# Three small edits late in a hybrid attention, gated-linear-attention and convolution layer: which engine makes the low parts of the last four output weights, what four weight scalings are queued behind, and which engine does one scaling of the end

## The chip, the cores and the metric

One Trainium2 chip; the kernel runs on one of its cores. The time is the device time of one execution in microseconds. The executions shown of the kernel before took 885.99, 885.36 and 882.93 us, median 885.36. A further execution was recorded by the hardware profiler; rows and times inside the kernel are from that one, and are microseconds from the start of its span.

## The reference, cut to what matters

One layer over 512 latent tokens (width 1024) with 256 context tokens. The edits touch the output projection `w_out`, the weights of `w_down`, and the final RMSNorm.

```python
h = modulate(rms_norm(x_lat, norm1_g), sh1, sc1)
mix = token_mixer(h, hc, ...)            # ends in (g_mla*br_mla + g_gla*br_gla) @ w_out
x_lat = x_lat + gt1 * mix
h = modulate(rms_norm(x_lat, norm2_g), sh2, sc2)
val, gate = split(h @ w_up)              # 2 x 2816 columns
gate = depthwise_conv_3x3(gate) + conv_b
x_lat = x_lat + gt2 * ((gelu(gate) * val) @ w_down)
return rms_norm(x_lat, final_g)
```

## The kernel before

**Matrix products in three parts.** Every float32 operand is split into a high part, rounded to the narrower `F32R`, and a low part, the rest. `split` (line 141) does it with a cast on ScalarE and a subtraction on GpSimd or VectorE; `mm3` (146) multiplies high by high, high by low and low by high, so each product is three matmuls on TensorE.

**Who sets the order.** The code is written in the order of the mathematics. A scheduler then puts each engine's instructions into one fixed sequence, from its own estimate of when each becomes ready; on the chip an engine works through its sequence and waits at an instruction whose inputs are not there. `tc.issue_after(x)` tells the scheduler to put what is traced in its block behind `x` on the engine of `x`; instructions of the block on other engines get no such rule. Loads are issued by SyncE's queue (SP), in order as well. A load waits there until the last reader of the buffer that it overwrites is done: three buffers `raw`, two `rawd`, and four pairs `whi`/`wlo` of split weights, which TensorE frees by finishing with them.

**The output projection** (lines 1359 to 1450). `load_wo` loads eight blocks of 128 rows of `w_out` (k = 0 to 7) and splits each into its own pair of tiles `s`. Blocks 4 to 7 are the last; their low parts are made by GpSimd for 4 and 6, by VectorE for 5 and 7. `w_out_norm(t)` then multiplies them with the 128 tokens of tile t, adds the result to the residual (`x`), normalizes it into `xn`, and `transposed(t, xn)` turns `xn` on TensorE and makes `h` for the MLP.

**The down projection** (lines 1570 to 1680). Eighteen of the 22 blocks of `w_down` go through a Strassen-like scheme in nine pairs (n = 0 to 8). For each n, the loop at 1619 loads and splits two weight tiles, `wa` and `wb`, and does 24 matmuls (`product`, 1581). The other four blocks (`last`) are multiplied plainly at the end; before that each is scaled by `gt2` and split. These four scalings stand in the loop's passes n = 1, 2, 4 and 5 in an `issue_after` block behind `done[0]`, a matmul, while the block holds work for VectorE and ScalarE alone. After the loop come the sums `u1`, `u2`, `u7`, `c22` and nine passes of `back`, whose first weights (`back_weights(0)`) are traced at n = 6.

**The end** (lines 1710 to 1762). For each tile t of 128 tokens: twelve matmuls per half with the four `last` blocks, the residual added from PSUM on VectorE, squares on ScalarE with their sum, the product with the gain `fg` on GpSimd, a reciprocal root `r2`, and a scaling of each half of 512 columns by `r2`. Tile 3 is cut into 512, 256 and 256 columns, the last quarter in a bank of its own.

Of the kernel before, what the change touches and what calls it, by code (L numbers as in the profile page):

```python
# [13 lines left out]
ALU = mybir.AluOpType  # L14
# [58 lines left out]
def block_kernel(ctx: ExitStack, tc: tile.TileContext, p, out):  # L73
# [3 lines left out]
    class Engine:  # L77
# [5 lines left out]
        def __getattr__(self, op):  # L83
            fn = getattr(self.eng, op)

            def call(*args, **kw):
                if self.name in behind:
                    with tc.issue_after(behind[self.name].ins):
# [6 lines left out]
    V, A, G, PE, SY = (Engine("V", nc.vector), Engine("A", nc.scalar), Engine("G", nc.gpsimd),  # L95
                       Engine("PE", nc.tensor), Engine("SY", nc.sync))
    cnt = [0]

    def tl(pool, shape, dt, tag, bufs=None):
        cnt[0] += 1  # L100
        kw = {} if bufs is None else {"bufs": bufs}
        return pool.tile(shape, dt, name=f"{tag}_{cnt[0]}", tag=tag, **kw)
# [8 lines left out]
    def pb():  # L111
        return tl(psp, [128, 512], F32, "pb", 4)
# [4 lines left out]
    def S4(shape, dt=F32R):  # L117
        return tl(s4, shape, dt, "s4")

    def S4f():  # L120
        return S4([128, 1024], F32)

    def sm(n, tag, bufs=2):
        return tl(small, [128, n], F32, tag, bufs)
# [4 lines left out]
    def whl():  # L129
        return tl(st, [128, 1024], F32R, "whi", 4), tl(st, [128, 1024], F32R, "wlo", 4)  # L130

    def f(ap):
        return ap.bitcast(F32)

    def tt(eng, out_, a, b, op):
        return eng.tensor_tensor(out=out_, in0=a, in1=b, op=op)

    def sub(eng, out_, a, b):
        eng.tensor_tensor(out=out_, in0=a, in1=b, op=ALU.subtract)

    def split(hi, lo, src, eng=None):

        A.copy(hi, src)
        sub(eng or G, lo, src, f(hi))

    def mm3(o, sh, sl, mh, ml, first, last):
        PE.matmul(o, lhsT=sh, rhs=mh, start=first, stop=False)
        PE.matmul(o, lhsT=sh, rhs=ml, start=False, stop=False)
        return PE.matmul(o, lhsT=sl, rhs=mh, start=False, stop=last)
# [67 lines left out]
    def split_w(r, n=1024, eng=None):  # L217
        h, l = whl()
        split(h[:, 0:n], l[:, 0:n], r[:, 0:n], eng)
        return h, l  # L220
# [125 lines left out]
    with tc.tile_pool(name="e1", bufs=1) as e1:  # L346
# [324 lines left out]
        for j in range(1, 8):  # L671
            n = j + 1
# [351 lines left out]
        for k in range(2):  # L1024
            V.scalar_tensor_tensor(out=kc[:, 256 * k:256 * k + 256], in0=cb_[k], scalar=col("kv_norm_g", k),
                                   in1=rb[:, 0:256], op0=ALU.mult, op1=ALU.mult)
# [332 lines left out]
    def load_wo(k, tile_=raw_tile):  # L1359
        r = tile_()  # L1360
        load[0] = SY.dma_start(out=r, in_=w_out[:, k, :])
        h_, l_ = S4([128, 1024]), S4([128, 1024])
        split(h_, l_, r, V if k in (5, 7) else G)
        wo.append((h_, l_))

    def up_weights(i):
        return split_w(load_cols(w_up, FF + i * 128)), split_w(load_cols(w_up, i * 128))
# [8 lines left out]
    with tc.tile_pool(name="emg", bufs=1) as em_:  # L1376
# [9 lines left out]
        for j in range(8):  # L1386
# [16 lines left out]
            if j in (1, 2, 3, 5):  # L1403
                load_wo(len(wo), mraw)
# [76 lines left out]
        for c0 in (FF + 256, 256):  # L1481
            h_, l_ = S4([128, 1024]), S4([128, 1024])
# [13 lines left out]
    with tc.tile_pool(name="eff", bufs=1) as ef:  # L1496
# [55 lines left out]
        for i in range(3, NF):  # L1552
            w = up_weights(i)
            ps = (pb(), pb())
# [9 lines left out]
            n = (i - 4) // 2  # L1564
# [10 lines left out]
        def raw_():  # L1575
            raws[0] += 1
            return raw_tile() if raws[0] % 5 in (1, 2, 3) else tl(ef, [128, 1024], F32, "rawd", 2)

        done = [None]

        def product(ps, hl, c, w, b, start, stop):
            for t in range(2):
                cs, bs = slice(c + t * 128, c + t * 128 + 128), slice(b, b + 512)
                done[0] = mm3(ps[t], hl[0][:, cs], hl[1][:, cs], w[0][:, bs], w[1][:, bs], start, stop)

        def halves(z):
            return [z[:, 0:512], z[:, 512:1024]]
# [31 lines left out]
        for n in range(NP):  # L1619
            r = raw_()  # L1620
            SY.dma_start(out=r[:, 0:512], in_=w_down[:, 2 * n, 0:512])
            SY.dma_start(out=r[:, 512:1024], in_=sums_[n][:, 1536:2048])
            wa = split_w(r, eng=G if n < 2 else V)
            r = raw_()
            SY.dma_start(out=r, in_=sums_[n][:, 0:1024])
            wb = split_w(r, eng=G if n < 2 else V)
            a, z = n == 0, n == NP - 1
            product(p1, first[n], 0, wa, 0, a, z)
            product(p6, first[n], 768, wa, 512, a, z)
            product(p7, first[n], 512, wb, 512, a, z)  # L1630
            product(p5, first[n], 256, wb, 0, a, z)
            if n == 0:
                for k in range(NF - NL, NF):
                    last.append(S4f())
                    load[0] = SY.dma_start(out=last[-1], in_=w_down[:, k, :])
            elif n in (1, 2, 4, 5):
                r = last[len(wl_)]
                with tc.issue_after(done[0].ins):
                    tt(V, r, r, gt2, ALU.mult)
                    wl_.append((S4([128, 1024]), S4([128, 1024])))  # L1640
                    split(*wl_[-1], r, V)
            if n == NP - 3:
                bw.append(back_weights(0))
# [58 lines left out]
        def down(k, t, half, w, a=0, n=512):  # L1702
            cs, hs = slice(t * 128, (t + 1) * 128), slice(half * 512 + a, half * 512 + a + n)
            mm3(acc[t][half][:, a:a + n], hid[k][:, 0, cs], hid[k][:, 1, cs], w[0][:, hs], w[1][:, hs], k == NF - NL,
                k == NF - 1)

        def residual(t, a, b, ps):
            tt(V, x2[t][:, a:b], x2[t][:, a:b], ps, ALU.add)

        for t in range(4):  # L1710
            last = t == 3
            o_t = S4f()
            parts = [(0, 512), (512, 768), (768, 1024)] if last else [(0, 512), (512, 1024)]
            ss = sm(len(parts), f"ssf{len(parts)}")
            if not last:
                for half in range(2):
                    for n in range(NL):
                        down(NF - NL + n, t, half, wl_[n])
            for i, (a, b) in enumerate(parts):
                if not last:  # L1720
                    residual(t, a, b, acc[t][i])
                elif i == 0:
                    for n in range(NL):
                        down(NF - NL + n, t, 0, wl_[n])
                    residual(t, a, b, acc[t][0])
                elif i == 1:
                    for n in range(NL):
                        down(NF - NL + n, t, 1, wl_[n], 0, 256)
                    residual(t, a, b, acc[t][1][:, 0:256])
                else:  # L1730

                    cs = slice(t * 128, (t + 1) * 128)
                    rest = pb()[:, 0:256]
                    for n in range(NL):
                        hd, w = hid[NF - NL + n], wl_[n]
                        mm3(rest, hd[:, 0, cs], hd[:, 1, cs], w[0][:, a:b], w[1][:, a:b], n == 0, n == NL - 1)
                    residual(t, a, b, rest)
                if last and i == 2:
                    V.scalar_tensor_tensor(out=o_t[:, a:b], in0=x2[t][:, a:b], scalar=1.0, in1=x2[t][:, a:b], op0=ALU.mult,
                                           op1=ALU.mult, accum_out=ss[:, i:i + 1])  # L1740
                else:
                    A.activation(o_t[:, a:b], x2[t][:, a:b], AF.Square, accum_out=ss[:, i:i + 1])
                if not last or i == 0:
                    tt(G, x2[t][:, a:b], x2[t][:, a:b], fg[:, a:b], ALU.mult)
            s1 = sm(1, "ssg")
            tt(V, s1, ss[:, 0:1], ss[:, 1:2], ALU.add)
            if last:
                V.tensor_scalar(out=s1, in0=s1, scalar1=-0.5 / D, scalar2=-0.5 * EPS, op0=ALU.mult, op1=ALU.add)
                v = sm(1, "rv1")
                V.scalar_tensor_tensor(out=v, in0=ss[:, 2:3], scalar=-0.5 / D, in1=s1, op0=ALU.mult, op1=ALU.add)  # L1750
                r2 = rstd_exp(None, 1, None, v)
            else:
                r2 = rstd_exp(s1, 1, 1.0 / D)
            for i in range(2):
                hs = slice(512 * i, 512 * i + 512)
                if last and i == 1:
                    V.scalar_tensor_tensor(out=x2[t][:, hs], in0=x2[t][:, hs], scalar=r2, in1=fg[:, hs], op0=ALU.mult,
                                           op1=ALU.mult)
                elif t == 2:
                    V.tensor_scalar(out=x2[t][:, hs], in0=x2[t][:, hs], scalar1=r2, scalar2=None, op0=ALU.mult)  # L1760
                else:
                    A.activation(x2[t][:, hs], x2[t][:, hs], AF.Copy, scale=r2)
                (A if last and i == 0 else SY).dma_start(out=out[0, t * 128:(t + 1) * 128, hs], in_=x2[t][:, hs])
# [24 lines left out]
```

## Time and profile before

| what | before |
|---|---|
| time of the executions shown | 885.99, 885.36, 882.93 us (median 885.36) |
| time of the profiled execution | 884.84 us |
| its span | 882.9 us |
| mean granted TensorE clock | 0.997 |
| ScalarE (ACT), GpSimd (POOL) busy | 47%, 44% of the span |
| VectorE (DVE) busy | 73% of the span |

The profiled execution's time is 1.9 us more than its span, which runs from the first to the last instruction. In a row of the timeline stand the start, the duration, the engine, line and operation, the tile written and those read, a count of merged instructions, and in square brackets how long the engine stood idle before it and what it waited for. PE is TensorE, SPq the queue that issues loads. Nearly all rows carry line 90, the helper that records every instruction, so tiles tell the instructions apart: `s` is a tile of the large pool, `p` and `pb` are PSUM tiles.

### The profile page before, as it was taken

The numbers are of one execution on the slowest core, as the hardware profiler recorded it, in microseconds if no ns is written. First come the engines' busy times: TensorE is split into PE (matmuls) and PEld (weight loads), VectorE is DVE, ScalarE is ACT, GpSimd is POOL, SyncE is SP. The second block draws the span as 40 slices with busy tenths as digits, with TensorE's granted clock in tenths as the row PEclk, the third lists the DMA queues.
The fourth block names the chain that finished last, engine by engine and source line by source line (L and its number), as shares of the span: only waits on it lengthen the run. The fifth ranks groups of instructions, "written<-read, shape, count | busy, mean of one in ns | idle before, by whom it ended". The sixth has DMA issues, their size and how long they took to land.

```text
span 882.9 us, 12813 instructions
## 1 busy us (share of the span) xinstructions
PE 866.2 (98%) x4794; PEld 737.3 (83%) x4794; DVE 645.3 (73%) x1049; ACT 413.5 (47%) x666; POOL 385.3 (44%) x258
## 2 busy tenths in 40 slices
PE   7999999999999999999999999999999999999996
PEld 6788899888888888888887889888888888878885
DVE  4477788885978787985676684976677665787856
ACT  4455766773354545444544433333334333365414
POOL 2512355460524252434563422777767776400004
PEclk9999999999999999999999999999999999999998
DMA  9970001207414333536981721656546755588502
GB/s 294 320 183 1 1 4 33 73 27 213 107 37 131 109 108 84 168 107 217 288 275 56 225 96 37 227 180 193 188 142 194 225 181 158 163 278 271 212 12 95
DMA packets 141648, 130.53 MB, mean 148 GB/s; under 512 B 7947, under 2 KB 122995, under 8 KB 141586
## 3 DMA queue, kind: packets, MB, share of 16 engines
q1 hardware_dynamic: 140354, 126.67, 47.0%
q10 hardware_dynamic: 832, 2.40, 0.7%
q8 instruction: 37, 0.61, 0.3%
q0 software_dynamic: 400, 0.65, 0.3%
q14 instruction: 25, 0.20, 0.1%
HBM read 115.87 MB, written 13.63 MB: 147 GB/s over the span
## 4 chain that ended last, share of the span: by engine, by line
PE 86%; DVE 3%; DMA 3%; issue 3%; POOL 2%; ACT 2%; SPq 0%; POOLq 0%; DVEq 0%; ACTq 0%
PE pb L90 46%; PE p L90 20%; PE pb L89 14%; PE p L89 6%; DMA raw<-in_w_ada_dram 2%; POOL wlo L90 1%; DVE s L90 1%; POOL s L90 1%; DMA s<-in_w_down_dram 1%; ACT P L90 1%; DVE mx L90 1%; DVE kT L90 0%; ACT ph L90 0%; ACT s L90 0%; DVE P L90 0%
## 5 line engine op out<-in xcount | busy, mean ns | idle before, releaser
L90 POOL TENSOR_TENSOR wlo<-raw,whi 128x1024 fp32r<-128x1024 f32 (+1 forms) x91 | 210.9, 2325 | 217.8 <-ACT whi L90 187.3
L90 PE MATMUL pb<-s,whi 128*128 128x512 f32 (+1 forms) x906 | 271.6, 382 | 0.0
L90 PEld LDWEIGHTS pb<-s,whi 128*128 128x128 f32 x906 | 167.4, 188 | 32.0
L90 PE MATMUL pb<-s,wlo 128*128 128x512 f32 (+1 forms) x453 | 172.9, 382 | 0.0
L90 ACT CAST whi<-raw 128x1024 fp32r<-128x1024 f32 (+1 forms) x106 | 102.9, 975 | 123.6 <-PE pb L90 56.2
L90 DVE SCALAR_TENSOR_TENSOR ac<-pb,cwT,ac 128x441 f32<-128x441 f32 (+2 forms) x160 | 110.9, 694 | 13.6 <-ACT ac L90 9.3
L89 PE MATMUL pb<-s,whi 128*128 128x512 f32 x320 | 101.3, 394 | 0.0
L90 PEld LDWEIGHTS pb<-s,wlo 128*128 128x128 f32 x453 | 85.2, 188 | 16.4
L90 PE MATMUL p<-s,s 128*128 128x512 f32 (+1 forms) x398 | 84.2, 365 | 1.2 <-POOL s L90 0.6
L90 PEld LDWEIGHTS p<-s,s 128*128 128x128 f32 x398 | 67.0, 189 | 13.8 <-DVE s L90 1.3
L89 PEld LDWEIGHTS pb<-s,whi 128*128 128x128 f32 x320 | 59.3, 188 | 11.5
L89 PE MATMUL pb<-s,wlo 128*128 128x512 f32 x160 | 62.9, 393 | 0.0
L90 PE MATMUL p<-whi,s 128*128 128x512 f32 x168 | 55.9, 394 | 0.0
L90 PE MATMUL pb<-whi,s 128*128 128x512 f32 x164 | 53.5, 391 | 0.0
L90 POOL TENSOR_TENSOR s<-s,edge 128x512 f32<-128x512 f32 x7 | 10.5, 1504 | 93.8 <-ACT s L90 93.8
L90 PE MATMUL pb<-s,s 128*32 128x128 f32 (+2 forms) x340 | 46.1, 319 | 0.7 <-DMA s<-in_w_ada_dram 0.7
L90 ACT ACTIVATE ac<-ac 128x512 f32<-128x512 f32 x22 | 13.9, 632 | 70.3 <-DVE ac L90 70.1
L90 DVE TENSOR_TENSOR pl<-pb,ph 128x512 fp32r<-128x512 f32 x48 | 33.0, 687 | 13.0 <-ACT ph L90 12.5
L90 PE MATMUL p<-kT,s 128*128 128x512 f32 (+1 forms) x192 | 41.2, 351 | 0.9 <-ACT P L90 0.9
L90 PEld LDWEIGHTS pb<-s,s 128*128 128x128 f32 (+1 forms) x340 | 36.1, 159 | 6.6 <-DVE rv L90 1.1
L90 PE MATMUL p<-s,whi 128*128 128x256 f32 (+1 forms) x156 | 38.6, 339 | 0.0
L90 ACT CAST ph<-pb 128x512 fp32r<-128x512 f32 x48 | 28.2, 587 | 20.7 <-PE pb L90 20.6
(274 smaller groups left out, 1670.8 us busy)
## 6 DMA issues: line engine op xcount, KB each, us to landing
raw<-in_w_up_dram SPq DMA_DIRECT2D x44, 512.0 KB, 4.8
raw<-in_w_in_dram SPq DMA_DIRECT2D x28, 512.0 KB, 4.1
rawd<-in_w_down_dram SPq DMA_DIRECT2D x22, 512.0 KB, 5.2
s<-in_w_ada_dram SPq DMA_DIRECT2D x20, 512.0 KB, 6.4
ws<-rawd SPq DMA_DIRECT2D x18, 512.0 KB, 5.7
raw<-in_w_ada_dram SPq DMA_DIRECT2D x10, 512.0 KB, 7.7
xn<-in_w_ada_dram SPq DMA_DIRECT2D x10, 512.0 KB, 5.3
wa<-in_w_ada_dram SPq DMA_DIRECT2D x8, 512.0 KB, 5.3
```

Of the source, the lines that this page charges most:

```text
L89: return fn(*args, **kw)
L90: ins = fn(*args, **kw)
```

## The change

Three edits, and what follows from them in the order.

```diff
     def sub(eng, out_, a, b):
-        eng.tensor_tensor(out=out_, in0=a, in1=b, op=ALU.subtract)
+        return eng.tensor_tensor(out=out_, in0=a, in1=b, op=ALU.subtract)
 
     def split(hi, lo, src, eng=None):
         A.copy(hi, src)
-        sub(eng or G, lo, src, f(hi))
+        return sub(eng or G, lo, src, f(hi))
...
         h_, l_ = S4([128, 1024]), S4([128, 1024])
-        split(h_, l_, r, V if k in (5, 7) else G)
+        split(h_, l_, r, V if k > 3 else G)
         wo.append((h_, l_))
...
             r = raw_()
             SY.dma_start(out=r, in_=sums_[n][:, 0:1024])
-            wb = split_w(r, eng=G if n < 2 else V)
+            wb = whl()
+            low = split(*wb, r, G if n < 2 else V)
...
-            elif n in (1, 2, 4, 5):
+            elif n in (3, 4, 6, 7):
                 r = last[len(wl_)]
-                with tc.issue_after(done[0].ins):
+                with tc.issue_after(low.ins):
                     tt(V, r, r, gt2, ALU.mult)
                     wl_.append((S4([128, 1024]), S4([128, 1024])))
                     split(*wl_[-1], r, V)
...
-                elif t == 2:
+                elif t == 2 and i == 0:
                     V.tensor_scalar(out=x2[t][:, hs], in0=x2[t][:, hs], scalar1=r2, scalar2=None, op0=ALU.mult)
                 else:
                     A.activation(x2[t][:, hs], x2[t][:, hs], AF.Copy, scale=r2)
```

**First place: the output projection.** On VectorE, `s_801`, `s_804`, `s_807` and `s_810` are the low parts of blocks 4, 5, 6 and 7:

```order
 L90 TENSOR_TENSOR s_403_2384<-s_403_2384,p_798_4747 128x512
 L90 TENSOR_TENSOR s_796_4739<-sg_4733,s_796_4739 128x512
+L90 TENSOR_TENSOR s_801_4757<-raw_4754,s_800_4756 128x1024
 L90 TENSOR_TENSOR s_804_4763<-raw_4760,s_803_4762 128x1024
+L90 TENSOR_TENSOR s_807_4769<-raw_4766,s_806_4768 128x1024
 L90 TENSOR_TENSOR s_403_2384<-s_403_2384,p_798_4747 128x512
 L90 TENSOR_TENSOR s_810_4775<-raw_4772,s_809_4774 128x1024
```

Two subtractions of 128x1024 have come to VectorE, ahead of and behind the one that was there; GpSimd has lost the same two. On TensorE, at the same place (`p_819` is token tile 0, `p_825` tile 1, `s_806` and `s_807` the high and low part of block 6):

```order
 L90 MATMUL p_819_4786<-s_806_4768,s_787_4674 128x512
+L90 MATMUL p_819_4786<-s_807_4769,s_787_4674 128x512
+L90 MATMUL p_819_4786<-s_806_4768,s_787_4674 128x512 x2
+L90 MATMUL p_819_4786<-s_807_4769,s_787_4674 128x512
+L90 MATMUL p_819_4786<-s_806_4768,s_787_4674 128x512
 L90 MATMUL p_825_4852<-s_718_4311,s_703_4230 128x512
 L90 MATMUL p_825_4852<-s_719_4312,s_703_4230 128x512
```

The rest of block 6 for tile 0 is now done at once, where thirteen matmuls of tile 1 stood ahead of it. Behind this, block 7 of tile 0 is finished five matmuls sooner, and the transposes of tile 0 stand five matmuls sooner.

**Second place: VectorE in the loop over n.** Before, from the low part of n = 2's `wa` (`wlo_7241`) on; `gt_404` marks the four scalings, `wlo_7247` is n = 2's `wb`, `wlo_7283` and `wlo_7289` are n = 3's two:

```order
L90 TENSOR_TENSOR wlo_7241<-rawd_7237,whi_7240 128x1024
L90 TENSOR_TENSOR s_1115_7137<-ac_7125,s_1115_7137 128x512
L90 TENSOR_TENSOR s_1129_7187<-s_1129_7187,gt_404_2389 128x1024
L90 TENSOR_TENSOR wlo_7247<-raw_7244,whi_7246 128x1024
L90 TENSOR_TENSOR s_1130_7189<-s_1130_7189,gt_404_2389 128x1024
L90 TENSOR_TENSOR s_1140_7234<-s_1129_7187,s_1139_7233 128x1024
L90 TENSOR_TENSOR s_1131_7191<-s_1131_7191,gt_404_2389 128x1024
L90 TENSOR_TENSOR wlo_7283<-raw_7279,whi_7282 128x1024
L90 TENSOR_TENSOR wlo_7289<-raw_7286,whi_7288 128x1024
L90 TENSOR_TENSOR s_1132_7193<-s_1132_7193,gt_404_2389 128x1024
```

After, from the same place; `wlo_7236` and `wlo_7242` are n = 2, `wlo_7273` and `wlo_7279` n = 3, `wlo_7315` and `wlo_7321` n = 4, `wlo_7357` n = 5:

```order
L90 TENSOR_TENSOR wlo_7236<-rawd_7232,whi_7235 128x1024
L90 TENSOR_TENSOR s_1115_7137<-ac_7125,s_1115_7137 128x512
L90 TENSOR_TENSOR wlo_7242<-raw_7239,whi_7241 128x1024
L90 TENSOR_TENSOR wlo_7273<-raw_7269,whi_7272 128x1024
L90 TENSOR_TENSOR wlo_7279<-raw_7276,whi_7278 128x1024
L90 TENSOR_TENSOR s_1129_7187<-s_1129_7187,gt_404_2389 128x1024
L90 TENSOR_TENSOR wlo_7315<-rawd_7311,whi_7314 128x1024
L90 TENSOR_TENSOR s_1152_7308<-s_1129_7187,s_1151_7307 128x1024
L90 TENSOR_TENSOR wlo_7321<-rawd_7318,whi_7320 128x1024
L90 TENSOR_TENSOR s_1130_7189<-s_1130_7189,gt_404_2389 128x1024
L90 TENSOR_TENSOR wlo_7357<-raw_7353,whi_7356 128x1024
```

No scaling stands ahead of n = 3's low parts any more; the four are spread behind the second low part of n = 3, 4, 6 and 7. On SP's queue the two loads of `back_weights(0)` have moved back as well: its block of `w_down` behind the load for `back_weights(1)`, and its stored sums behind the first sums of `back_weights(2)`.

**Third place: VectorE at the end.** `s_1208` is tile 2, `s_1209` tile 3, `ssg` and `ssf` its sums of squares:

```order
-L90 TENSOR_SCALAR s_1208_7549<-s_1208_7549,rr_1283_7979 128x512 x2
+L90 TENSOR_SCALAR s_1208_7549<-s_1208_7549,rr_1283_7979 128x512
 L90 TENSOR_TENSOR s_1209_7550<-s_1209_7550,pb_7852 128x256
+L90 TENSOR_TENSOR ssg_8037<-ssf_1287_7992 128x1
 L90 TENSOR_TENSOR s_1209_7550<-s_1209_7550,pb_8022 128x256
-L90 TENSOR_TENSOR ssg_8037<-ssf_1287_7992 128x1
+L90 TENSOR_SCALAR ssg_8037<-ssg_8037 128x1
 L90 SCALAR_TENSOR_TENSOR s_1286_7991,ssf_1287_7992<-s_1209_7550 128x256
-L90 TENSOR_SCALAR ssg_8037<-ssg_8037 128x1
```

One of two scalings of tile 2 is gone from VectorE, and stands on ScalarE between tile 3's first square and its second. The sum of the first two squares now stands ahead of the last addition from PSUM.

More of the change, by code (lines that the diff above doesn't have):

```diff
@@ L1577, in raw_ @@
             return raw_tile() if raws[0] % 5 in (1, 2, 3) else tl(ef, [128, 1024], F32, "rawd", 2)
-        done = [None]
         def product(ps, hl, c, w, b, start, stop):
@@ L1583, in product @@
                 cs, bs = slice(c + t * 128, c + t * 128 + 128), slice(b, b + 512)
-                done[0] = mm3(ps[t], hl[0][:, cs], hl[1][:, cs], w[0][:, bs], w[1][:, bs], start, stop)
+                mm3(ps[t], hl[0][:, cs], hl[1][:, cs], w[0][:, bs], w[1][:, bs], start, stop)
         def halves(z):
```

## The prediction

> **What bounds the kernel now.** I read the busy shares first, then TensorE's waits by releaser, then its timeline around each.
>
> ```profile
> span 882.9 us, 12813 instructions
> PE 866.2 (98%) x4794; PEld 737.3 (83%) x4794; DVE 645.3 (73%) x1049; ACT 413.5 (47%) x666; POOL 385.3 (44%) x258
> PE p L90 <- DVE s L90: 2.5, 2, 2.1
> PE p L90 <- DVE wlo L90: 0.9, 1, 0.9
> PE p L90 <- POOL s L90: 0.6, 1, 0.6
> 668.40 97.95 PE pb L90 x432
> ```
>
> TensorE is busy 98% of the span, so only its idle time and what stands behind its last matmul can go. Of the three waits only the last two (total, times, longest) lie where the change reaches. The last row, from the chain of waits, gives the undisturbed pace: 97.95 / 432 = 0.227 us from one matmul's start to the next. A row of n matmuls without a break thus takes (n - 1) x 0.227 plus the last one's own 0.39 us.
>
> **First part: the low parts of blocks 4 and 6.**
>
> ```profile
> 478.81 2.94 ACT L90 CAST s<-raw 128x1024 fp32r<-128x1024 f32 x3
> 479.93 2.39 POOL L90 TENSOR_TENSOR s<-raw,s 128x1024 fp32r<-128x1024 f32 x1 [8.03 <-ACT s L90]
> 480.83 2.57 DVE L90 TENSOR_TENSOR s<-raw,s 128x1024 fp32r<-128x1024 f32 x1 [1.21 <-ACT s L90]
> 481.37 0.39 PE L90 MATMUL p<-s,s 128*128 128x512 f32 x1
> 482.37 20.26 PE L90 MATMUL p<-s,s 128*128 128x512 f32 x88 [0.61 <-POOL s L90]
> 775.87 1.23 DVE L90 TENSOR_TENSOR wlo<-rawd,whi 128x1024 fp32r<-128x1024 f32 x1 [1.67 <-ACT whi L90]
> ```
>
> The three casts of blocks 4 to 6 start at 478.81 and end about 0.95 apart, the first at 479.9. GpSimd makes block 4's low part until 482.32, and TensorE, due at 481.37 + 0.23 = 481.60, starts at 482.37: 0.77 late. The idle figure in brackets is smaller, because a matmul counts as busy for 0.39 and the next starts after 0.23. The 88 matmuls take 20.26 where 87 x 0.227 + 0.39 = 20.14 were due, so restarting costs another 0.1. Loss: 0.9.
>
> VectorE stands idle from 479.6 to 480.83 (the 1.21 in its row) and needs 1.23 for such a subtraction, as the sixth row shows. With the change it does block 4 from 479.9 to 481.1, block 5 to 482.3, block 6 to 483.4. TensorE needs them at 481.6, 483.0 and 484.3 (6 and 12 matmuls after the first): slacks of 0.5, 0.7 and 0.9. **The 0.9 goes.** GpSimd's two subtractions of 2.39 leave a queue that nothing else waits in here.
>
> [...]
>
> What is late next? Block 7's cast, and the transposes of tile 0, five matmuls sooner now.
>
> ```profile
> 483.43 0.33 SPq L90 DMA_DIRECT2D raw<-in_w_out_dram  x1
> 487.04 1.05 ACT L90 CAST s<-raw 128x1024 fp32r<-128x1024 f32 x1 [5.29 <-DMA raw<-in_w_out_dram]
> 490.04 10.38 POOL L90 TENSOR_TENSOR wlo<-raw,whi 128x1024 fp32r<-128x1024 f32 x4 [4.38 <-ACT whi L90]
> 493.50 4.66 DVE L90 TENSOR_TENSOR x<-x,xn 128x512 f32<-128x512 f32 x2
> 500.66 0.75 DVE L90 TENSOR_SCALAR xn<-x,rr 128x1024 f32<-128x1024 f32 x1
> ```
>
> Block 7's load left at 483.43, when VectorE released block 5's buffer, and was cast 3.6 later. Now it takes block 4's buffer at 481.1, so its cast ends near 485.8; TensorE reaches it 26 matmuls after 481.60, at 487.5. Its low part is ready near 487.1 against 488.9. The transposes come 83 matmuls after 481.60, at 500.4. `xn` was ready at 501.41; the two additions ahead of it took 4.66 because GpSimd's four subtractions ran beside them. These now start some 1.6 sooner, since their loads wait for buffers that come free 1.6 to 2.3 sooner; so `xn` moves to about 499.8. The slack of 0.6 is the smallest that this edit leaves, and I take no loss; the worst is one more GpSimd operation in the way, 2.4.
>
> **Second part: the four scalings.**
>
> ```profile
> 777.92 1.23 DVE L90 TENSOR_TENSOR s<-s,gt 128x1024 f32<-128x1024 f32 x1 [0.22 <-DMA s<-in_w_down_dram]
> 779.06 1.22 DVE L90 TENSOR_TENSOR wlo<-raw,whi 128x1024 fp32r<-128x1024 f32 x1
> ...
> 782.47 1.22 DVE L90 TENSOR_TENSOR s<-s,gt 128x1024 f32<-128x1024 f32 x1
> 783.60 1.22 DVE L90 TENSOR_TENSOR wlo<-raw,whi 128x1024 fp32r<-128x1024 f32 x1
> 780.14 1.99 ACT L90 CAST whi<-raw 128x1024 fp32r<-128x1024 f32 x2
> 782.94 1.07 PE L90 MATMUL pb<-whi,s 128*128 128x512 f32 x4
> 784.88 0.50 PE L90 MATMUL p<-wlo,s 128*128 128x512 f32 x1 [0.87 <-DVE wlo L90]
> ```
>
> From 777.92 VectorE works without a gap, 1.14 from start to start, and reaches n = 3's first low part at 783.60, though its cast ended at 781.2. Ahead of it stand three scalings and one low part of theirs. TensorE was due at 782.94 + 4 x 0.227 = 783.85 and starts at 784.88: 1.03 late, and this first matmul takes 0.50 instead of 0.39. Loss: 1.1.
>
> With the new order VectorE goes on from n = 2's second low part to n = 3's. VectorE was done with the instruction before at 777.92 - 0.22 = 777.7; less the 0.9 of the first part, it starts at 776.8, and n = 3's two end at 779.2 and 780.3. TensorE needs them as the 74th and 86th matmul of the loop, where 783.85 was the 79th: at 783.85 - 5 x 0.227 - 0.9 = 781.8 and at 784.5. Their casts, no longer behind the cast of a scaled weight, wait only for buffers that n = 1 has left. Slack: over 2.
>
> ```profile
> 794.00 1.99 ACT L90 CAST whi<-raw 128x1024 fp32r<-128x1024 f32 x2
> 794.75 1.54 PE L90 MATMUL pb<-whi,s 128*128 128x512 f32 x5
> ```
>
> A second, hidden loss: these five matmuls take 1.54 where 4 x 0.227 + 0.39 = 1.30 were due, while the cast that they need ends at 795.0: 0.2. That cast (n = 5's `wb`) stood behind casts of scaled weights and moves up too. From n = 4 on, each new pair is limited by its buffers, which TensorE frees 36 matmuls (8.2) ahead of their next use; a cast and a low part need 1.0 + 1.2, and a scaling and a low part of a scaled weight between add 2.4. So **1.3 goes** in this part.
>
> **Third part: the end.**
>
> ```profile
> 864.14 11.19 PE L90 MATMUL pb<-s,s 128*128 128x512 f32 x60
> 873.73 0.49 DVE L90 TENSOR_SCALAR s<-s,rr 128x512 f32<-128x512 f32 x1
> 874.13 1.52 DVE L90 TENSOR_SCALAR s<-s,rr 128x512 f32<-128x512 f32 x1
> 875.57 0.74 DVE L90 TENSOR_TENSOR s<-s,pb 128x256 f32<-128x256 f32 x2
> 876.63 0.42 DVE L90 SCALAR_TENSOR_TENSOR s<-s 128x256 f32<-128x256 f32 x1
> 877.15 0.16 DVE L90 SCALAR_TENSOR_TENSOR rv<-ssf,ssg 128x1 f32<-128x1 f32 x1
> 874.02 1.34 POOL L90 TENSOR_TENSOR s<-s,edge 128x512 f32<-128x512 f32 x1 [1.43 <-ACT s L90]
> 871.13 1.32 ACT L90 ACTIVATE s<-s,rr 128x512 f32<-128x512 f32 x2
> 873.22 0.63 ACT L90 ACTIVATE s<-s 128x512 f32<-128x512 f32 x1 [0.44 <-DVE s L90]
> 876.01 0.42 ACT L90 ACTIVATE s<-s 128x256 f32<-128x256 f32 x1 [2.06 <-DVE s L90]
> ```
>
> TensorE ends at 875.33; the rest is one chain. VectorE's second scaling takes 1.52, against 0.49 for the first, as GpSimd works from 874.02 to 875.36. So tile 3's next addition, whose matmuls ended near 873.9 (12 x 0.12 before the end), starts at 875.57, its square on ScalarE at 876.01, and `rv` at 877.15. Without that scaling the addition starts at 874.13. ScalarE, free at 873.9, does the scaling in 0.7 (1.32 / 2) and the square until 875.1. The last addition then waits for TensorE alone, 875.35 to 875.7, the last square follows, and `rv` comes at 875.7 + (877.15 - 876.63) = 876.25. **0.9 goes.** No more than 875.57 + 0.37 - 875.33 = 0.6 of the addition's own delay plus the 0.3 between its end and 876.63 can. If ScalarE's scaling came late, its cost would be at most 0.7 of that.
>
> [...]
>
> **Sum.** 0.9 + 1.3 + 0.9 = 3.1, or with the losses unrounded (0.77 + 0.12, 1.03 + 0.11 + 0.24, 0.9) 3.2. TensorE is gapless between the places, so nothing swallows a shift. The profiled execution's 884.84 becomes 881.6; it lies 0.5 below the median shown, 885.36, on which I forecast: **882.2**, or 0.36% less.
>
> **Rivals.** *(A) The first part gives nothing*: `xn`, with 0.6 of slack, comes late because GpSimd's subtractions start when they did; the transposes then wait 0.9 or so. For it: the 4.66; against: the buffers come free sooner. 883.1. *(B) The second part turns into another wait*: casts and low parts of n = 4 to 8 come late, since four scalings still share VectorE. For it: 10 us of VectorE without a gap; against: the slack of two. 883.5. *(C) The end gives half or less*, ScalarE being late, or the chain held by the last load's way out: 882.7. *(D) Nothing moves*, three hidden waits in place of the three: 885.4.
>
> *(E) Slower: the loads of* `back_weights(0)`.
>
> ```profile
> 792.05 0.90 SPq L90 DMA_DIRECT2D s<-ws  x2
> 797.71 1.05 ACT L90 CAST s<-s 128x1024 fp32r<-128x1024 f32 x1 [1.72 <-DVE wlo L90]
> ```
>
> Their second half was issued at 792.05 and cast at 797.71, 5.7 later. Now it is queued behind a load that waits for n = 7's second low part, near 800.3, and leaves near 801. Its cast stands on ScalarE ahead of two weight casts, one more of the tied weights and the copies that free PSUM for `back`, 5 to 6 us of work that must end near 814.5. It decides from a landing past 808.5, 7.5 after issue; against the 5.7 seen that is 2 of slack. To be slower by over 0.3% in all, it must land 5.9 later still; the medians of the page's loads say no. At 13 us: 888.1.
>
> **How the numbers follow.** About 0.3% (2.7) is what a measurement of this kernel can tell from no change. Forecast 0.64, A 0.11, B 0.09, C 0.08, D 0.05, E 0.03. The forecast lies only 0.5 beyond 882.7, where "faster" begins, and the three executions shown spread over 3, so I give it 0.7 faster, 0.3 the same; A, B and C 0.35 faster; D and a little of B to slower with E. Faster 0.55, same 0.40, slower 0.05. Range: below, the sum with 1.8 of the spread, 880.4; above, D less a little, 885.2.
>
> **What would show it.** Right: no wait of TensorE for GpSimd's `s` near 482 and none for `wlo` near 784; VectorE's block 5 in 1.23; five matmuls near 794 in 1.30; `rv` 0.9 after TensorE's end instead of 1.8. Wrong: a wait for `xn` at the first transposes near 500, for `whi` or `wlo` between 782 and 814, or for ScalarE's copies near 814; ScalarE's square of tile 3 later than 875 less the shift.

## The result, and the profile after

The changed kernel took 882.71 us (median of 22 executions, 881.81 to 886.16), the kernel before 885.72 in the same rounds (22 executions, 882.93 to 889.57). The ratio is 0.9967, with a 95% interval of 0.9955 to 0.9979: 3.0 us less, where 3.2 was forecast. The gain is clear of zero, but the interval also holds gains below the 0.3% from which the prediction speaks of "faster". The profiled executions lie 2.4 apart in span. The page of the changed kernel:

```profile
span 880.5 us, 12812 instructions
PE 865.7 (98%) x4794; PEld 737.0 (84%) x4794; DVE 646.1 (73%) x1050; ACT 414.2 (47%) x667; POOL 379.6 (43%) x256
```

TensorE's waits by releaser in the changed kernel, from 450 to 884 us (total, times, longest), are a single row; the rows for GpSimd's `s` and VectorE's `wlo` are gone, and this one is new:

```profile
PE pb L90 <- DVE ac L90: 0.5, 1, 0.5
```

Its timeline (start, duration, engine, tile written and read, idle time before), at the places that the prediction spoke of:

```profile
478.32 2.94 ACT L90 CAST s<-raw 128x1024 fp32r<-128x1024 f32 x3
479.40 3.50 DVE L90 TENSOR_TENSOR s<-raw,s 128x1024 fp32r<-128x1024 f32 x3 [0.26 <-ACT s L90]
481.30 19.24 PE L90 MATMUL p<-s,s 128*128 128x512 f32 x84
...
744.12 0.70 PE L90 MATMUL pb<-s,whi 128*128 128x512 f32 x2 [0.52 <-DVE ac L90]
...
777.58 3.49 DVE L90 TENSOR_TENSOR wlo<-raw,whi 128x1024 fp32r<-128x1024 f32 x3
802.15 0.86 SPq L90 DMA_DIRECT2D s<-ws  x2
807.21 1.05 ACT L90 CAST s<-s 128x1024 fp32r<-128x1024 f32 x1 [1.80 <-DMA s<-ws]
...
867.57 6.21 PE L90 MATMUL pb<-s,s 128*128 128x512 f32 x38
872.18 0.49 DVE L90 TENSOR_SCALAR s<-s,rr 128x512 f32<-128x512 f32 x1
872.30 0.71 ACT L90 ACTIVATE s<-s,rr 128x512 f32<-128x512 f32 x1
873.82 0.42 DVE L90 TENSOR_TENSOR s<-s,pb 128x256 f32<-128x256 f32 x1
874.74 0.16 DVE L90 SCALAR_TENSOR_TENSOR rv<-ssf,ssg 128x1 f32<-128x1 f32 x1
```

The three low parts of `w_out` follow each other on VectorE at 1.14, and TensorE runs through 84 matmuls in 83 x 0.227 + 0.39 = 19.2. In the loop over n three low parts of weights stand together from 777.58, and the chain of waits from 774 to 800 is TensorE alone:

```profile
by line: PE pb L90 54.0%; PE p L90 47.2%
```

At the end `rv` comes 874.74 - (867.57 + 6.21) = 0.96 after TensorE, instead of 1.82. Matmul by matmul, the changed kernel is 0.97 earlier than before behind 482 (0.07 of it from ahead of that place), only 0.17 behind 744, 1.55 behind 795, and 2.4 at `rv`. So in this pair the three parts paid 0.90, 1.38 and 0.87, and a wait that the kernel before did not have took 0.68 and a restart of 0.1 back. The experiments ask two things: whether each part is worth what one pair of profiles says, and whether that wait belongs to the change.

### The profile page after: what moved, and what is told of

Read it like the earlier page. It is cut to its first block, busy times and chain, and to the rows that moved or that the text cites. A ratio compares the mean times of both kernels' runs of the same rounds, so it can differ in the third digit from the quotient of the medians.

```text
span 880.5 us, 12812 instructions
## 1 busy us (share of the span) xinstructions
PE 865.7 (98%) x4794; PEld 737.0 (84%) x4794; DVE 646.1 (73%) x1050; ACT 414.2 (47%) x667; POOL 379.6 (43%) x256
## 4 chain that ended last, share of the span: by engine, by line
PE 86%; DMA 4%; DVE 4%; POOL 3%; ACT 2%; issue 1%; SPq 0%; DVEq 0%; POOLq 0%; ACTq 0%
PE pb L90 44%; PE p L90 22%; PE pb L89 14%; PE p L89 6%; DMA raw<-in_w_ada_dram 2%; DMA rawd<-in_w_down_dram 2%; POOL wlo L90 2%; DVE s L90 1%; ACT s L90 1%; ACT P L90 1%; DVE mx L90 1%; DVE ac L90 0%; POOL rawd L90 0%; SPq L90 0%; DVE kT L90 0%
```

## The experiments

Every profile, of experiments as well, runs the same 4,794 matmuls, so lateness is read at the same matmul each time. "Late" is a matmul's start after the one before it, less the undisturbed 0.23 (0.12 near 236, where matmuls are half as wide). L is the lead at 482: from the start of ScalarE's cast of block 4 to the time at which TensorE wants block 4. "150" is what 150 matmuls of the loop over n took from 776 on (at 0.2267 each, 34.0). e5, e5b, e6, e8 and e9 were executed once each, under the profiler: their traces are read here, and their times are not compared.

| run | block 4 by | L | late 482 | late 236 | late 744 | late at n = 3 | 150 | `rv` behind last matmul's end |
|---|---|---|---|---|---|---|---|---|
| before | GpSimd | 2.79 | 0.78 | 0 | 0 | 1.03 | 35.41 | 1.82 |
| after | VectorE | 3.20 | 0 | 0 | 0.68 | 0 | 34.03 | 0.96 |
| e1_wout_only | VectorE | 3.24 | 0 | 1.97 | 1.61 | 0.81 | 35.03 | 1.82 |
| e2_tie_only | GpSimd | 3.65 | 0 | 0 | 1.14 | 0 | 34.00 | 1.83 |
| e3_tail_only | GpSimd | 3.71 | 0 | 2.05 | 0 | 0.94 | 35.65 | 0.96 |
| e4_after_again | VectorE | 2.12 | 0.24 | 2.02 | 0 | 0 | 34.00 | 0.96 |
| e5_place_only | GpSimd | 3.56 | 0.03 | 1.97 | 0 | 0.56 | 34.89 | 1.83 |
| e5b_tie_early | GpSimd | 2.64 | 0.92 | 2.00 | 0.35 | 0 | 34.03 | 1.83 |
| e6_tail_no_pool | GpSimd | 3.09 | 0.49 | 1.98 | 0.97 | 1.23 | 35.52 | 1.03 |
| e7_last_sums_pool | VectorE | 3.02 | 0 | 0 | 0.55 | 0 | 34.05 | 0.96 |
| e8_last_sums_later | VectorE | 2.42 | 0 | 0 | 0 | 0 | 34.00 | 0.96 |
| e9_gate_split_v | VectorE | 3.46 | 0 | 0 | 0 | 0 | 34.00 | 0.96 |
| e10_both | VectorE | 4.17 | 0 | 0 | 0 | 0 | 34.00 | 0.96 |
| e11_after_third | VectorE | 3.18 | 0 | 2.10 | 1.34 | 0 | 34.00 | 0.96 |

**Each part alone, and the changed kernel once more.**

```diff
e1_wout_only, against before:
-        split(h_, l_, r, V if k in (5, 7) else G)
+        split(h_, l_, r, V if k > 3 else G)
e2_tie_only: the edits in the loop over n alone (passes 3, 4, 6, 7, behind low.ins)
e3_tail_only, against before:
-                elif t == 2:
+                elif t == 2 and i == 0:
```

> The kernel before with the first edit alone: the low parts of w_out's blocks 4 and 6 go to VectorE. My theory, from the row of 0.77 late and 0.12 of restart: TensorE's matmuls from the seventh of w_out on start 0.9 to 1.0 earlier than in the kernel before, there is no wait for GpSimd's s near 482, and the first transposes near 500 do not wait. Rival 1 (GpSimd and VectorE hinder each other, moving work between them gives nothing): shift 0 at 490. Rival 2 (the MLP loop is paced by its loads, so what is gained at 482 is handed back at a wait for VectorE's ac near 744, as the profiled execution of the changed kernel shows 0.7 of it): shift about -0.9 at 500 to 700, and about -0.2 after 750, time within 0.3 of the kernel before. Theory without rival 2: -0.9 in the time, ratio 0.999.

> The kernel before with the second edit alone: scalings and splits of the last four weights after n = 3, 4, 6, 7, tied behind VectorE's own low parts. Theory: no wait of TensorE for wlo near 784, the five matmuls near 795 in 1.3 instead of 1.54, so TensorE is 1.3 to 1.4 earlier from there to its last matmul, nothing changed before 780, time -1.3 (ratio 0.9985). Rival (the lateness moves to another whi or wlo between 786 and 814): 0 to 0.6. A wait for VectorE's ac near 744 as in the changed kernel: by chance of the loads it may come here too, though nothing before 780 was changed; if it is a consequence of the first edit's earlier start it does not.

> The kernel before with the third edit alone: one of the two scalings of tile 2 at the end goes back to ScalarE. Theory (the 1.52 of VectorE's second scaling is on the chain to the end): rv comes 0.9 to 1.0 instead of 1.8 after TensorE's last matmul, time -0.9, ratio 0.999. [...] TensorE's shift is 0 all through.

> The changed kernel once more. If the wait for VectorE's ac near 744 (0.68 of TensorE's time in the profiled execution) is chance of the loads, it is absent or of another size or at another place here; if it follows from the change (0.97 earlier at 482, while the loads of the MLP loop keep their own pace), it comes back at the same place with 0.5 to 0.9. Time 882.7 against 885.7 of the kernel before, ratio 0.9967; with the wait gone in all executions it would be 0.996.

In times, to the kernel before: e1 1.0000 (0.9982 to 1.0018), e2 0.9988 (0.9968 to 1.0009), e3 1.0008 (0.9990 to 1.0026), the changed kernel again 0.9984 (0.9964 to 1.0004). Each interval is 3 to 4 us wide, more than any part is worth, so the times can't tell the parts from nothing (e3's holds its 0.999 only at the edge, and its profile has the wait near 236, which the kernel before lacks in its own); the traces can.

e1 has the low part as forecast and starts behind 482 as early, against the matmuls ahead, as the changed kernel; what it does not have is a gain in time: TensorE's waits from 450 to 884 in e1 are

```profile
PE pb L90 <- DVE ac L90: 1.4, 1, 1.4
PE p L90 <- DVE wlo L90: 0.7, 1, 0.7
```

The wait for `ac` is the new wait again, twice as long. By e1 alone the second rival (what is gained at 482 is handed back at 744) would stand. The table speaks against it: e2, e5b and e6 have the wait without the first edit, e4 and e9 have the edit without the wait. It comes in 6 of the 11 profiles up to e11 that leave this place as it was. It averages 0.73 in the five of these with the edit, 0.41 in the six without; that the edit makes it a little longer is not excluded by so few.

e2 and e3 hold the surprise: GpSimd makes block 4 as before, and TensorE is not late at 482. In e2 (the kernel before, but for the loop over n):

```profile
477.76 2.94 ACT L90 CAST s<-raw 128x1024 fp32r<-128x1024 f32 x3
478.88 5.75 POOL L90 TENSOR_TENSOR s<-raw,s 128x1024 fp32r<-128x1024 f32 x2 [8.04 <-ACT s L90]
```

The cast starts 3.65 ahead of TensorE's need instead of 2.79. In the kernel before TensorE started 482.37 - 478.81 = 3.56 after the cast's start; with VectorE it could start 479.40 + 1.23 + 0.05 - 478.32 = 2.36 after it. So TensorE should be late by 3.56 - L with GpSimd and by 2.36 - L with VectorE, or not at all. This stands in the expectations of most of the later runs, and it holds in all of them to 0.03: e5b, with L = 2.64, is late by 0.92. Its rows on ScalarE, GpSimd and TensorE:

```profile
480.79 2.95 ACT L90 CAST s<-raw 128x1024 fp32r<-128x1024 f32 x3
481.92 2.38 POOL L90 TENSOR_TENSOR s<-raw,s 128x1024 fp32r<-128x1024 f32 x1 [8.04 <-ACT s L90]
484.36 1.89 PE L90 MATMUL p<-s,s 128*128 128x512 f32 x7 [0.76 <-POOL s L90]
```

By these two formulas GpSimd would be late by 0.46 on average over the fourteen leads (0 to 1.44) and VectorE by 0.02. The difference is an estimate of what the first part is worth.

**The loop over n: the place or the tie?**

```diff
e5_place_only, against before (still behind a matmul):
-            elif n in (1, 2, 4, 5):
+            elif n in (3, 4, 6, 7):
e5b_tie_early, against e2_tie_only (other passes):
-            elif n in (3, 4, 6, 7):
+            elif n in (2, 3, 4, 5):
```

> The kernel before with the four scalings moved to n = 3, 4, 6, 7 but still tied behind a matmul, so not behind VectorE's own low parts. Theory (the tie does it: without it VectorE still takes the scalings before the low parts of n = 3): TensorE again starts 0.8 to 1.0 late at the first matmul of n = 3 (start to start 1.0 to 1.3 instead of 0.23), as in the kernel before (1.26), e1_wout_only (1.04) and e3_tail_only (1.16). Rival (the later place alone does it): 0.23 there, as in e2_tie_only. At 482 no edit is made, so by the lead of ScalarE's cast of block 4 over the matmul that needs it (L, from the cast's start to that matmul's due time) TensorE is late by 3.56 - L or not at all; the kernel before had L = 2.79 and 0.77, e2_tie_only L = 3.65 and 0, e3_tail_only L = 3.71 and 0.

> The second edit alone, with the scalings one pass of n earlier (n = 2, 3, 4, 5 instead of 3, 4, 6, 7) and tied behind VectorE's own low parts. Theory (order on VectorE decides, not the distance): no wait of TensorE for wlo near 784, as in e2_tie_only; the scaling after n = 2 stands ahead of the low parts of n = 3 and takes 2.4 of a slack of over 2, so at most 0.3 late there. Rival (the later place was needed too): 0.5 to 1.0 late near 784. At 482 as in the kernel before: late by 3.56 - L or not at all.

e5 on VectorE, and then the matmul of n = 3 on TensorE:

```profile
780.41 1.23 DVE L90 TENSOR_TENSOR s<-s,gt 128x1024 f32<-128x1024 f32 x1 [0.54 <-DMA s<-in_w_down_dram]
781.55 1.22 DVE L90 TENSOR_TENSOR wlo<-raw,whi 128x1024 fp32r<-128x1024 f32 x1
782.68 1.22 DVE L90 TENSOR_TENSOR s<-s,gt 128x1024 f32<-128x1024 f32 x1
783.82 1.22 DVE L90 TENSOR_TENSOR s<-s,s 128x1024 fp32r<-128x1024 f32 x1
784.96 1.22 DVE L90 TENSOR_TENSOR s<-s,gt 128x1024 f32<-128x1024 f32 x1
786.09 2.36 DVE L90 TENSOR_TENSOR wlo<-raw,whi 128x1024 fp32r<-128x1024 f32 x2
...
787.37 0.50 PE L90 MATMUL p<-wlo,s 128*128 128x512 f32 x1 [0.40 <-DVE wlo L90]
```

These are the same operations in the same order as before: three scalings (`gt`) and one of their low parts ahead of n = 3's. The later place changed nothing, since a block tied behind a matmul leaves VectorE free. That TensorE is late by 0.56 and not by the 0.8 to 1.0 expected is a matter of VectorE's lead: its run begins at 780.41, 6.40 ahead of the time at which TensorE wants n = 3's low part, and in the kernel before at 777.92, 5.93 ahead. In all five profiles with this order, lead and lateness add up to 6.95 or 6.96, so this loss too is a need minus a lead. e5b has the scalings earlier than the change has them, tied, and is not late at all (34.03). The tie does it: late by 0.56 to 1.23 in the five profiles without it, by 0 in the nine with it.

**The end: is it GpSimd that makes the 1.52?**

```diff
e6_tail_no_pool, against before:
-                if not last or i == 0:
+                if not last:
...
-                if last and i == 1:
+                if last:
```

> The kernel before, with both scalings of tile 2 at the end still on VectorE, but GpSimd's last product with the final norm's weights taken away (tile 3's first half is scaled and multiplied on VectorE in one instruction, as its second half is). Theory (GpSimd's work beside it makes the second scaling 1.52 instead of 0.49): the second scaling takes 0.5 and rv comes 1.2 to 1.3 after the last matmul's start, as with the third edit (1.24), instead of 2.1. After rv VectorE has one more product, so the end itself gains less. Rival (the 1.52 is its own, for example the second half's place in memory or a wait that the row does not show): 1.52 stays, and rv 2.1.

e6 on VectorE, and TensorE's last matmuls:

```profile
878.37 0.88 DVE L90 TENSOR_SCALAR s<-s,rr 128x512 f32<-128x512 f32 x2
881.00 0.16 DVE L90 SCALAR_TENSOR_TENSOR rv<-ssf,ssg 128x1 f32<-128x1 f32 x1
...
876.71 3.26 PE L90 MATMUL pb<-s,s 128*128 128x512 f32 x25
```

Both scalings take 0.88 together, where the kernel before had 1.92, and `rv` comes 1.03 after TensorE's end. Ahead of these scalings and beside them nothing else was changed: GpSimd's product beside it makes the second scaling long.

**The wait near 744.** `ac` is a sum that VectorE builds for the depthwise convolution, by eight products for each block that read PSUM (`ac<-pb,cwT,ac`); TensorE waits near 744 for the last of the eight. In the changed kernel VectorE stands still for the loads of the last pair of weights to be summed (`rawd`), ahead of these products:

```profile
732.72 0.69 DVE L90 TENSOR_TENSOR rawd<-rawd 128x512 f32<-128x512 f32 x1 [4.35 <-DMA rawd<-in_w_down_dram]
733.33 0.68 DVE L90 TENSOR_TENSOR second<-pb,ac 128x512 f32<-128x512 f32 x1
...
739.60 4.37 DVE L90 SCALAR_TENSOR_TENSOR ac<-pb,cwT,ac 128x441 f32<-128x441 f32 x6
```

The products end at 743.97, and TensorE, due at 743.44, starts at 744.12. The first subtraction starts at 732.72, in the kernel before at 732.81, while TensorE wants the products 0.97 sooner than there: in this pair of profiles the wait takes back most of the gain from 482, because the load was there no sooner.

```diff
e7_last_sums_pool, against the changed kernel:
-            sub(V if n else G, b11, b12, b11)
-            sub(V if n else G, b12, b22, b12)
+            sub(V if 0 < n < NP - 1 else G, b11, b12, b11)
+            sub(V if 0 < n < NP - 1 else G, b12, b22, b12)
e8_last_sums_later, against the changed kernel:
...
+                elif n == NP - 1 and i % 2:
+                    with tc.issue_after(mark[0].ins):
+                        weight_subs(n, made)
...
```

In e8, for the last pair alone, `weight_subs` holds the four subtractions, and `mark` is VectorE's split of that pair's first sum; the loads stay where they were.

> The changed kernel with the two first subtractions of the last pair of summed weights on GpSimd instead of VectorE, so that VectorE does not stand still for their loads near 728 to 736 (3.1 to 5.3 in all six profiles so far). Theory (that standstill makes VectorE late with the value part near 744, where TensorE waited 0.68 in the changed kernel, 1.61 in e1_wout_only, 1.14 in e2_tie_only and 0 in the three others): no wait of TensorE for ac or rawd there, time 0.5 to 0.7 below the changed kernel on average, ratio to before 0.996 to 0.997. Rival (the casts and sums that follow on GpSimd come later instead): a wait of TensorE for whi or wlo of the last pair near 808 to 815, 0.5 or more. At 482, with VectorE doing block 4: late by 2.36 - L or not at all (the changed kernel L = 3.20 and 0; its second execution L = 2.12 and 0.24).

> The changed kernel with all four subtractions of the last pair of summed weights issued behind VectorE's split of that pair's first sum, instead of ahead of it, so that neither VectorE nor GpSimd stands at their loads ahead of work that the next value part waits for. Theory (the wait for VectorE's ac near 744 comes from this standstill; in e7_last_sums_pool it only moved to GpSimd): VectorE has no wait for a load between 725 and 745, its ac near 744 is ready 2 or more earlier than TensorE needs it, and TensorE has no wait between 700 and 775. Rival (VectorE is behind there for its own work alone): a wait for ac near 744 of 0.3 or more stays. At 482, with VectorE doing block 4: late by 2.36 - L or not at all.

e7 (ratio 0.9985, 0.9966 to 1.0004) keeps the wait: 0.55 near 744, and 0.57 more near 773. Its theory fell. On GpSimd and VectorE:

```profile
732.12 1.29 POOL L90 TENSOR_TENSOR rawd<-rawd 128x512 f32<-128x512 f32 x1 [5.53 <-DMA rawd<-in_w_down_dram]
733.37 0.74 POOL L90 TENSOR_TENSOR edge<-edge,second 128x256 f32<-128x256 f32 x1
...
737.16 2.33 DVE L90 TENSOR_TENSOR s<-edge,s 128x1024 fp32r<-128x1024 f32 x1 [5.67 <-ACT s L90]
```

Now GpSimd stands 5.53 for the load, `edge` stands behind it, and VectorE waits 5.67 for what is made of `edge`. The standstill had only changed engines. e8 puts the four subtractions behind that work, and VectorE there has no wait for a load:

```profile
727.93 0.69 DVE L90 TENSOR_TENSOR second<-pb,ac 128x512 f32<-128x512 f32 x1 [0.76 <-ACT ac L90]
731.38 3.14 DVE L90 TENSOR_TENSOR s<-edge,s 128x1024 fp32r<-128x1024 f32 x1 [0.43 <-ACT s L90]
734.45 0.68 DVE L90 TENSOR_TENSOR rawd<-rawd 128x512 f32<-128x512 f32 x1
...
736.24 3.65 DVE L90 SCALAR_TENSOR_TENSOR ac<-pb,cwT,ac 128x504 f32<-128x504 f32 x5
```

The products end at 739.89, 3.3 ahead of TensorE's need at 743.19, and TensorE waits nowhere from 700 to 775. One profile without the wait would say little, since five of eleven lack it without this edit; the size of the wait says more. In these eleven, TensorE is late by 10.05 less the time by which the second of VectorE's subtractions (`rawd<-rawd,rawd`) starts ahead of TensorE's need, or not at all, to 0.05 each; in each of them VectorE had stood 3.1 to 5.3 for the load just ahead of these subtractions. The wait near 744 comes from work queued behind a load on an engine that works in order, and its length from when the load lands. In the kernel before, the same sum gives 0.2 to spare, so its profile hid the wait.

**Two more edits together, beside the changed kernel.** The wait near 236 (last section) was taken up as well: six of the ten profiles until then have it (in the end 7 of the 12 that leave that place as it was).

```diff
e9_gate_split_v, against the changed kernel:
-            wr = split_w(load_cols(w_in, CGR + h * 128))
+            wr = split_w(load_cols(w_in, CGR + h * 128), eng=V if h == 0 else G)
e10_both: the edits of e8 and e9
e11_after_third: the changed kernel
```

> The changed kernel with one subtraction near 231 (the low parts of the first gate's weights) moved from GpSimd to VectorE. Six of ten profiles have TensorE wait 1.8 to 1.9 for VectorE's mp near 236, four have none, and in three of the six the granted clock then fell to 0.57 to 0.67 over the next 4 and cost another 1.6. Theory (VectorE's multiplications of 0.48 take 2.6 beside GpSimd's run of four subtractions, and it depends on some 0.3 of a load's landing whether a gap between the third and the fourth lets one through): with one of the four gone there is always a gap of over 2, so no wait for mp. Rival (VectorE's chain is late for its own loads): the wait of 1.8 stays in six of ten executions. One profile can only speak against the theory by showing the wait.

> The changed kernel with the edits of e8_last_sums_later and e9_gate_split_v together. Theory: neither wait (near 236 and near 744) in the profile; over executions 0.6 x 2.0 + 0.3 x 1.6 = 1.7 less from the first and 0.5 less from the second than the changed kernel, so ratio to before about 0.994 to 0.995 where the changed kernel has 0.997, and a smaller spread. Rival (the waits are only moved on): the same time as the changed kernel in this call.

> The changed kernel a third time, on the same chip and in the same rounds as e10_both. By the sum of the parts as the ten profiles show them (first part 0.46 on average, second 1.1 to 1.3, third 0.87) it should lie 2.4 to 2.6 below the kernel before, ratio 0.997. At 482: late by 2.36 - L or not at all, for L the lead of ScalarE's cast of block 4.

Neither e9 nor e10 has the wait near 236. In time, beside the same kernel before: e11 883.72 (881.62 to 887.86), ratio 0.9958 (0.9937 to 0.9979); e10 881.84 (881.57 to 883.61), ratio 0.9948 (0.9925 to 0.9972). The lowest executions are alike, but six of e11's twelve lie above the highest of e10's eight: this fits waits that come in some executions and that e10 takes away. e10 is the fastest of the versions executed more than once, by 1.9 us in the medians; the two intervals overlap, so the size of this gain is not secured.

## Why the prediction held, step by step

**The sum.** 3.2 was forecast and 3.0 (1.9 to 4.0) measured. The other two comparisons with the kernel before give 1.4 (0.9984) and 3.7 (0.9958); the intervals of both hold 3.0. By the traces the parts are 0.5, 1.4 and 0.9, so 2.8. The forecast was high by the first term, and that 3.0 came so near to 3.2 is in part luck: the three comparisons differ by more than that term.

**First part, forecast 0.9: right in mechanism, mis-sized.** The order came as forecast, the slacks so or larger: three subtractions at 1.14, block 7 loaded at 480.65 (481.1 forecast), no wait at the transposes (`xn` was ready at 499.17, 1.2 ahead of them, where the prediction had a slack of 0.6), so (A) did not occur in any of eight profiles with the edit. What failed is the step from one profile to the median: 0.77 was the lateness of an execution with a lead of 2.79. Over fourteen leads the edit is worth 0.46 - 0.02 = 0.44, and up to 0.1 of restart. The prediction had the needed rows: it worked out that TensorE wanted block 4 at 481.60 and that ScalarE's cast began at 478.81, but did not ask what sets that cast, which hangs on a chain through VectorE behind a load (`xn` from `w_ada`: VectorE waits 1.85 for it until 454.68 before, 1.42 until 453.61 in e2). In all fourteen profiles the cast starts 24.1 to 24.2 after VectorE's first product with that load. Moving the two subtractions to VectorE paid where the lead was short: in e4 GpSimd would have been 1.44 late by the formula, VectorE was 0.24. Block 5's low part took VectorE 2.57 beside GpSimd before; in the changed kernel three follow each other at 1.14, and GpSimd starts its next low parts only at 487.79.

**Second part, forecast 1.38 in its terms: right.** The 150 matmuls take 35.41, 35.03, 35.65 and 35.52 in the four kernels without the second edit, 34.0 in all with the tie: 1.4. Counting e5 (34.89), which has the old order too, it is 1.3. Neither (B) nor a remaining wait appears. VectorE's run began 0.8 later than forecast (777.58 for 776.8), as the new wait near 744 had used up TensorE's lead; the slack of two covered it.

**Third part, forecast 0.9: right.** `rv` moved by 0.86 to 0.87 against TensorE's end in all profiles with the edit, and e6 shows that the cause is the one named. In the changed kernel the scaling of tile 2 that stays on VectorE takes 0.49, as before, and the other 0.71 on ScalarE (0.7 forecast); (C) did not occur.

**"TensorE is gapless between the places, so nothing swallows a shift"**: true of the profile that it was read from, not of the kernel. Waits near 236 and 744 come and go between executions, and one of them hid a quarter of the gain in the profile after.

**(E), the loads of** `back_weights(0)`: issued at 802.15 (801 forecast) and cast at 807.21, 5.1 later; the limit was 808.5 on the forecast's clock. Nothing was late. (By the prediction's own terms its 888.1 belongs to a landing 13.4 after issue, 7.5 + 5.9, and not 13.)

## What to carry to other kernels

A loss read from one profile is a sample: write it as what was needed minus a lead, and ask what sets the lead; if a load stands somewhere in its chain, the loss is different in each execution, and its mean can lie well below what was seen (0.46 against 0.77 here). A subtraction tied behind a matmul is not tied on VectorE (e5 still starts n = 3 late by 0.56, e2 by 0); what orders an engine's queue is a tie to an instruction of that engine. Work on data that may land late belongs behind the work that others wait for, and not merely on another engine, which then stands still in its place (GpSimd for 5.53 in e7).

## What the runs showed of the hardware

**Half a microsecond decides over two.** The wait near 236 is TensorE's for `mp`, which VectorE makes in small multiplications that take 0.48 by themselves, while GpSimd makes low parts. In the changed kernel, GpSimd, VectorE and TensorE:

```profile
226.25 7.35 POOL L90 TENSOR_TENSOR wlo<-raw,whi 128x1024 fp32r<-128x1024 f32 x3 [18.42 <-ACT whi L90]
234.10 2.43 POOL L90 TENSOR_TENSOR wlo<-raw,whi 128x1024 fp32r<-128x1024 f32 x1 [0.50 <-ACT whi L90]
228.72 8.09 DVE L90 SCALAR_TENSOR_TENSOR mp<-s,csilu,mp 128x256 f32<-128x256 f32 x4
234.45 0.50 PE L90 MATMUL pb<-ones,mp 128*128 128x1 f32 x4
```

The same code in its second execution (e4):

```profile
227.09 9.85 POOL L90 TENSOR_TENSOR wlo<-raw,whi 128x1024 fp32r<-128x1024 f32 x4 [18.41 <-ACT whi L90]
229.57 7.66 DVE L90 SCALAR_TENSOR_TENSOR mp<-s,csilu,mp 128x256 f32<-128x256 f32 x3
237.29 0.61 PE L90 MATMUL pb<-ones,mp 128*128 128x1 f32 x4 [1.86 <-DVE mp L90]
```

Beside a subtraction of GpSimd one multiplication of VectorE takes 2.6, so one gets through for each of GpSimd's. In the first execution GpSimd had a gap of 0.50 before its fourth, and the third of VectorE's four, which TensorE needs, ran in it undisturbed (four take 8.09); in the second, ScalarE's cast for the fourth came in time, there was no gap (three take 7.66), and TensorE started 2.0 late. What came earlier made the kernel slower. The border is sharp: with a gap of 0.25 (at 233.95) the kernel before had no wait, with 0.24 (at 233.51) e11 had it. In the twelve profiles that leave this place as it was, the cast for the fourth starts 1.72 to 1.96 ahead of TensorE's due time in the seven with the wait, 1.48 to 1.70 ahead in the five without. VectorE is held up beside GpSimd elsewhere too: the scaling of the end takes 1.52 beside GpSimd, 0.49 without. By what GpSimd holds it up, no run shows. With one of the four subtractions on VectorE (e9) nine multiplications run in 7.49:

```profile
229.45 3.49 DVE L90 TENSOR_TENSOR wlo<-raw,whi 128x1024 fp32r<-128x1024 f32 x1 [2.30 <-ACT whi L90]
233.12 7.49 DVE L90 SCALAR_TENSOR_TENSOR mp<-s,csilu,mp 128x256 f32<-128x256 f32 x9
```

**Behind a wait of under 2 TensorE's clock fell in three profiles of seven.** The window of e4 from 238 to 242 (busy times and counts of the engines, then granted clock, DMA share and GB/s):

```profile
238.00:242.00 4.00, 4.00 (x22) 4.00 (x22) 2.16 (x6) 0.09 (x1) 0.00 (x0) 0.57 0.50 131
```

Behind the 1.86 of waiting the granted clock is 0.57 there, where the first execution has 1.00, and the matmuls that follow lose another 1.6. The same happens in e5 (0.67, behind 1.82) and e6 (0.65, behind 1.82), and not in e1, e3, e5b and e11, whose waits are as long (1.81 to 1.94) and whose granted clock is 1.00 in each stretch of 2 us from 234 to 244. In the kernel before and the changed kernel, where TensorE stands idle for 0.9 at most at a time from 20 to 870 us, it is 1.00 in every microsecond of that time. What decides whether it falls behind such a wait, no run shows.
